# Summing the carry matrices' addends on VectorE, and making the second memory layer's operand earlier

## The chip, the cores and the metric

The kernel runs on one core of one Trainium2 chip. The core has a matrix engine (TensorE; PE in the profile, with its weight loads as PEld), a vector engine (VectorE, DVE), an activation engine (ScalarE, ACT), a general engine (GpSimd, POOL) and SyncE (SP), whose queue issues most transfers. Each engine works through its own instructions in order and waits for the others by semaphores. The metric is the device time of one execution, in microseconds; lower is better.

## The reference

One inference step of a two-layer streaming encoder. Layer 0 mixes tokens by an S5 state-space block, layer 1 by retention; each layer then attends to a memory and ends in a convolutional feed-forward block. Everything is float32. 512 prompt tokens and 32 sample tokens of width 1024 go through it. The change lies in two pieces:

```python
def s5_mixer(h, st_re, st_im, chunk, ...):
    a_bar, b_bar, c = s5_discretise(...)          # complex, 64 groups x 64 states
    ...
    # per group: x_t = a_bar * x_(t-1) + b_bar u_t ;  y_t = Re(c x_t) + d u_t
    g = jax.nn.gelu(y)
    out = g * jax.nn.sigmoid(g @ w_glu + b_glu)

def memory_kv(mem, g_mem, w_kv):                  # for each of the two layers
    m = rms_norm(mem, g_mem) @ w_kv               # mem: 256 tokens x 1024
    k, v = jnp.split(m, 2, axis=-1)
```

The memory keys and values of both layers depend on the memory tokens alone, and not on the encoder's progress.

## The kernel before, in words

The first stage (`phase1`) computes the S5 block and, between its parts, the memory keys and values of both layers. The stages after it (GLU, attention, feed-forward, retention, attention, feed-forward, final norm) aren't touched.

**S5.** The tokens are grouped by eight. Within eight tokens the recurrence is a matrix M per group; across them a carried state S is scanned. The 64 groups are handled in eight blocks of eight. For a block `e`, `powers` (letter V, line 813) makes operands on VectorE (lines 827 and 828) and GpSimd (829), `matrices` (M, 832) transposes them on TensorE (841), copies them by ScalarE (842), and builds M: Fg (853), copied into M by eight transfers (856). `states` (S, 858) multiplies the inputs on TensorE (867) and rotates the result on VectorE (882 to 886) and GpSimd. `scan` (Z, 892) runs the recurrence (900) and forms S (902 to 910); ScalarE copies its last columns out (912, 913). `carry` (C, 915) makes, for each half of a block, two products of 128x512 on VectorE, `y` (926) and `yt` (928): the two addends of the matrix by which the carried state is multiplied. `outputs` (O, 932) accumulates three products for each group on TensorE: M by the inputs (940), and S by `y` and by `yt` (942). ScalarE applies the activation (943), TensorE transposes (951), ScalarE copies the result into `g32` (953, 954).

**Memory keys and values.** `kv_units` (441) is a generator of 32 units, 16 for each layer: eight of keys (`keys`, 530) and eight of values (`values`, 553). Ahead of a layer's first unit stands `operand` (481): it loads the memory tokens in four transfers (450), and ScalarE scales them by the layer's gain. Layer 0's products are float32 (497, 528). Layer 1's operands are split into two parts that TensorE multiplies three times (240 to 242); its operand therefore takes eight ScalarE instructions (491) and eight VectorE instructions (492). Each unit loads a weight tile of 512 KB (520, or 226 with a rest that GpSimd's queue adds, 235).

**The order.** `fill(us)` draws units from the generator until their costs (3.5 us for each, 0 for an operand) have used up a credit. A prologue and then, for each block, a list written out by hand call the steps and fills in turn:

```python
PROLOGUE = (("V", 0), ("P", 0), ("M", 0), ("V", 1), ("S", 0), ("C", 0), ("Z", 0), ("M", 1), ("V", 2), ("F", 6))
ORDER = (("S", 1), ("C", 1), ("V", 3), ("Z", 1), ("O", 0), ("F", 4), ("M", 2), ("F", 5))
```

The number in ORDER is added to the block's. This gives priorities; a scheduler then fixes each engine's order ahead of the run, by its own estimate of times, and takes an instruction of lower priority first where the higher one isn't ready in that estimate. Most temporary tiles (the memory operands, `yt`, the products of V, S and Z, `g32`) come from one pool of 28 buffers of 560 columns (`slot`, 191). `y` comes from another of eight (`xl`, 807).

Of the kernel before, what the change touches and what calls it, by code (L numbers as in the profile page):

```python
# [13 lines left out]
OP = mybir.AluOpType  # L14
# [3 lines left out]
P = 128  # L18
# [7 lines left out]
NM = 256  # L26
# [146 lines left out]
class Kernel:  # L173
# [267 lines left out]
    def kv_units(self):  # L441

        nc, io = self.nc, self.io
        raw, first, ahead = [], [], []

        def load(ahead=lambda: None):
            raw.clear()
            for n in range(4):
                m = self.slot(512)
                nc.sync.dma_start(out=m, in_=io["memT"][n // 2][:, (n % 2) * 512:(n % 2 + 1) * 512])  # L450
                raw.append(m)
                if n == 1:
                    ahead()

        sq = []

        def squares():
            for k in range(4):
                t = self.slot(512)
                nc.scalar.activation(out=t, in_=raw[k], func=AF.Square)  # L460
                sq.append(t)
            for t, o in ((sq[0], sq[1]), (sq[2], sq[3]), (sq[0], sq[2]), (sq[0][:, :NM], sq[0][:, NM:])):
                nc.gpsimd.tensor_tensor(out=t, in0=t, in1=o, op=OP.add)

        def rms():

            ps = self.bank()
            for b in range(2):
                nc.tensor.matmul(ps[:, NM + b:NM + b + 1], lhsT=sq[0][:, b * P:(b + 1) * P], rhs=self.ones[:, :1], start=True, stop=True)
            self.mc = self.sp.tile([P, 2], F32, tag="mc", name="mc")  # L470
            m, tmp = self.small(2, "mm"), self.small(2, "mt")
            nc.vector.tensor_scalar(out=m, in0=ps[:, NM:NM + 2], scalar1=1.0 / D, scalar2=EPS, op0=OP.mult, op1=OP.add)
            self.rsqrt_of(m, self.mc, tmp)
            self.mps = ps

        def row():
            self.along_row(self.mps, self.mc, [(0, P), (1, P)])
            self.mr = self.sp.tile([P, NM], F32, tag="mr", name="mr")
            nc.scalar.copy(self.mr, self.mps[:, :NM])

        def operand(l):

            load(lambda: ahead.append(weights(0, io["w_k"][0, 0])) if l == 0 else None)
            self.mem = []
            for k in range(KT):
                src = raw[k // 2][:, (k % 2) * NM:(k % 2 + 1) * NM]
                g = self.gains[:, 32 + l * KT + k:33 + l * KT + k]
                if l in KV_SPLIT:
                    p = self.slot(2 * NM, dt=F32R)
                    m = p[:, :NM], p[:, NM:]  # L490
                    nc.scalar.activation(out=m[0], in_=src, func=AF.Copy, scale=g)
                    nc.vector.scalar_tensor_tensor(out=m[1], in0=src, scalar=g, in1=m[0].bitcast(F32), op0=OP.mult, op1=OP.subtract)
                else:
                    if k % 2 == 0:
                        t = self.slot(2 * NM)
                    m = t[:, (k % 2) * NM:(k % 2 + 1) * NM]
                    nc.scalar.activation(out=m, in_=src, func=AF.Copy, scale=g)
                self.mem.append(m)

        def staged():  # L500
            t = "acc" if self.n % 2 else "rr"
            return self.main.tile([P, T], F32, tag=t, bufs=1, name=self.name(t))

        def source(l, i):
            return io["w_k"][l, i] if i < KT else io["w_v"][l, (i - KT) // 4, (i - KT) % 4]

        prep = {}

        def look(u):

            if KT * 2 <= u + 1 < KT * 4:
                self.weights_close(prep[u + 1])
            if KT * 2 <= u + 2 < KT * 4:
                prep[u + 2] = self.weights_open(source(1, u + 2 - 2 * KT))

        def weights(l, src, u=None):
            if l in KV_SPLIT:
                return prep.pop(u)[:2]
            w = self.main.tile([P, 1024], F32, tag="wr", bufs=3, name=self.name("wr"))
            nc.sync.dma_start(out=w, in_=src)  # L520
            return w

        def product(l, out, a, ca, b, cb, k):

            if l in KV_SPLIT:
                self.mm3(out, [x[:, ca] for x in a], [x[:, cb] for x in b], k == 0, k == KT - 1)
            else:
                nc.tensor.matmul(out, lhsT=a[:, ca], rhs=b[:, cb], start=k == 0, stop=k == KT - 1)  # L528

        def keys(l, m):  # L530
            look(16 * l + m)
            w = ahead.pop() if ahead else weights(l, io["w_k"][l, m], 16 * l + m)
            ps = self.bank()
            for k in range(KT):
                product(l, ps[:, :NM], w, slice(k * P, (k + 1) * P), self.mem[k], slice(0, NM), k)
            first.append((l, m, ps))
            if l == 0 and m == 0:
                squares()
            if l == 0 and m == KV_RMS:
                rms()  # L540
            if l == 0 and m == KV_ROW:
                row()
            if l or m >= KV_ROW:
                for a in first:
                    keys_out(*a)
                first.clear()

        def keys_out(l, m, ps):
            o = staged()[:, :NM]
            nc.vector.tensor_tensor(out=o, in0=ps[:, :NM], in1=self.mr, op=OP.mult)  # L550
            nc.sync.dma_start(out=io["kT"][l, m // 4, :, (m % 4) * NM:(m % 4 + 1) * NM], in_=o)

        def values(l, n, c, ps):
            if c == 0:
                ps.extend([self.bank(), self.bank()])
            look(16 * l + 8 + 4 * n + c)
            w = weights(l, io["w_v"][l, n, c], 16 * l + 8 + 4 * n + c)
            for k2 in range(2):
                k = 2 * c + k2
                for b in range(2):  # L560
                    product(l, ps[b], self.mem[k], slice(b * P, (b + 1) * P), w, slice(k2 * 512, (k2 + 1) * 512), k)
            if c == 3:
                for b in range(2):
                    o = staged()[:, :512]
                    nc.scalar.activation(out=o, in_=ps[b], func=AF.Copy, scale=self.mc[:, b:b + 1])
                    nc.sync.dma_start(out=io["v"][l, b, :, n * 512:(n + 1) * 512], in_=o)

        for l in range(2):
            yield 0, lambda l=l: operand(l)
            for m in range(KT):  # L570
                yield KV_US, lambda l=l, m=m: keys(l, m)
            for n in range(2):
                ps = []
                for c in range(4):
                    yield KV_US, lambda l=l, n=n, c=c, ps=ps: values(l, n, c, ps)


    def cmul(self, eng, o, a, b, t, eng2=None):
# [10 lines left out]
    def phase1(self, sp):  # L589
        nc, io = self.nc, self.io  # L590
        V, A, PL = nc.vector, nc.scalar, nc.gpsimd
# [323 lines left out]
        def carry(e):  # L915

            d = E[e]
            g0 = 8 * e
            ca = load("ca", [P, 2, 8, C], io["ca"][e].rearrange("p (r n c) -> p r n c", r=2, n=8), 2)
            d["Y"] = []  # L920
            for hh in range(2):
                y, yt = xl(512), self.slot(512)
                y4, yt4 = (a.rearrange("p (g l c) -> p g l c", g=4, l=L) for a in (y, yt))
                shy = [P, 4, L, C]
                gg = slice(g0 + 4 * hh, g0 + 4 * hh + 4)
                V.tensor_tensor(out=y4, in0=ca[:, 0, 4 * hh:4 * hh + 4].unsqueeze(2).to_broadcast(shy),
                                in1=art[:, gg].unsqueeze(3).to_broadcast(shy), op=OP.mult)
                V.tensor_tensor(out=yt4, in0=ca[:, 1, 4 * hh:4 * hh + 4].unsqueeze(2).to_broadcast(shy),
                                in1=ait[:, gg].unsqueeze(3).to_broadcast(shy), op=OP.mult)
                d["Y"].append((y, yt))  # L930

        def outputs(e):
            d = E[e]
# [2 lines left out]
            for hh in range(2):  # L936
                py = self.bank()
                for i in range(4):
                    o, g = py[:69, i * P:(i + 1) * P], 4 * hh + i
                    nc.tensor.matmul(o, lhsT=u[:, g, 1:70], rhs=M[:, :, g], start=True, stop=False)  # L940
                    for n, y in enumerate(Y[hh]):
                        nc.tensor.matmul(o, lhsT=S[:, g, 0:69], rhs=y[:, i * P:(i + 1) * P], start=False, stop=n == 1)  # L942
                A.activation(out=yg[:, :, 64 * hh:64 * hh + 64].rearrange("p l (g c) -> p g l c", g=4),
                             in_=py[:69].rearrange("p (g l c) -> p g l c", g=4, l=8), func=AF.Gelu_apprx_tanh)
            g32 = self.slot()
# [469 lines left out]
```

## Time and profile before

| | us |
|---|---|
| median of three runs (1886.03 to 1888.63) | 1886.94 |
| the profiled execution | 1885.01 |
| its span in the trace | 1883.0 |
| TensorE busy in the span | 1823.7 |
| VectorE busy | 1055.0 |
| ScalarE busy | 629.0 |
| GpSimd busy | 342.3 |

The span runs from the first to the last instruction of the trace. Busy time is the time in which an engine had at least one instruction in work. In the timelines a row gives start and length in microseconds, the engine, the line of the kernel, the operation, the tile written and the tiles read, the shapes and how many instructions are merged into the row; square brackets at the end hold the idle time of the engine just ahead and what ended it. A row on TensorE counts passes: one float32 product is two.

### The profile page before, as it was taken

The page shows a single profiled execution, that of the slowest core. Times are in us where ns is not written, and L with a number is a line of the kernel's source. Part 1 is how long each engine was busy: PE and PEld are TensorE (multiplying, and loading weights), DVE is VectorE, ACT ScalarE, POOL GpSimd, SP SyncE. Part 2 cuts the span into 40 slices and gives each one's busy share as a digit, 9 for nine tenths or more (in the row PEclk, how much of TensorE's full clock was granted, in tenths as well). Part 3 has the DMA queues.
Part 4 walks back from the last instruction along what each step waited for, and adds up shares of the span by engine and source line. Part 5 has one row for each costly group of instructions (what it writes and reads, how often), then busy time and mean ns, then how long its engine had stood idle before and what let it go on. Part 6 is the DMA issues. An engine that isn't in the chain of part 4 may idle for free.

```text
span 1883.0 us, 33026 instructions
## 1 busy us (share of the span) xinstructions
PE 1823.7 (97%) x13943; PEld 1737.9 (92%) x13943; DVE 1055.0 (56%) x1779; ACT 629.0 (33%) x933; POOL 342.3 (18%) x416
## 2 busy tenths in 40 slices
PE   8778999999999999999999999999999999999998
PEld 7468799999999999999899899998899999999997
DVE  8887766545535535555555645556554554453553
ACT  3234454433323323333123222223443332232333
POOL 4645410021202202220000100100101121120221
PEclk9979999999999999999999999999999999999999
DMA  6637753122222222222222122222311222222221
GB/s 235 194 99 181 175 175 107 68 98 79 90 90 85 83 91 90 81 92 85 82 85 96 68 91 73 91 79 89 125 68 61 86 90 83 86 85 96 90 72 68
DMA packets 68276, 186.43 MB, mean 99 GB/s; under 512 B 9184, under 2 KB 18784, under 8 KB 68128
## 3 DMA queue, kind: packets, MB, share of 16 engines
q1 hardware_dynamic: 65536, 175.79, 28.1%
q0 software_dynamic: 2304, 8.39, 2.5%
q8 instruction: 109, 1.79, 0.4%
q14 instruction: 39, 0.32, 0.1%
q10 hardware_dynamic: 288, 0.15, 0.0%
HBM read 171.16 MB, written 10.77 MB: 97 GB/s over the span
## 4 chain that ended last, share of the span: by engine, by line
PE 88%; DVE 5%; DMA 2%; ACT 2%; issue 1%; POOL 1%; SPq 1%; DVEq 0%; ACTq 0%; POOLq 0%
PE ps L249 75%; PE ps L240 2%; PE ps L241 2%; PE ps L242 2%; PE bank L942 1%; PE bank L528 1%; DMA wr<-in_w_v 1%; DMA r<-in_memT 1%; PE ps L1339 1%; DVE wl L209 1%; PE bank L940 1%; POOL u L819 1%; PE ps L1328 0%; DMA wr<-in_w_k 0%; PE bank L742 0%
## 5 line engine op out<-in xcount | busy, mean ns | idle before, releaser
L249 PE MATMUL ps<-xh,wh 128*128 128x272 f32 x2432 | 505.7, 289 | 5.4 <-DVE x L372 3.5
L249 PE MATMUL ps<-xh,wl 128*128 128x272 f32 x2432 | 504.1, 289 | 0.0
L249 PE MATMUL ps<-xl,wh 128*128 128x272 f32 x2432 | 502.8, 288 | 0.0
L208 ACT CAST wh<-wr 128x1024 fp32r<-128x1024 f32 (+1 forms) x240 | 248.1, 1038 | 757.3 <-PE ps L249 639.7
L249 PE MATMUL ps<-r,wh 128*128 128x272 f32 x2688 | 447.8, 288 | 3.0 <-ACT r L954 1.6
L249 PEld LDWEIGHTS ps<-xh,wh 128*128 128x128 f32 x2432 | 382.4, 189 | 11.1 <-ACT r L314 3.7
L249 PEld LDWEIGHTS ps<-r,wh 128*128 128x128 f32 x2688 | 379.2, 188 | 6.4 <-ACT r L208 3.0
L249 PEld LDWEIGHTS ps<-xh,wl 128*128 128x128 f32 x2432 | 381.6, 189 | 2.3 <-issue 2.3
L249 PEld LDWEIGHTS ps<-xl,wh 128*128 128x128 f32 x2432 | 382.3, 188 | 0.3
L209 DVE TENSOR_TENSOR wl<-wr,wh 128x1024 fp32r<-128x1024 f32 (+1 forms) x240 | 296.2, 1237 | 93.2 <-ACT wh L208 85.2
L249 PE MATMUL ps<-r,wl 128*128 128x272 f32 x1344 | 277.7, 288 | 0.0
L249 PEld LDWEIGHTS ps<-r,wl 128*128 128x128 f32 x1344 | 210.6, 188 | 0.0
L372 DVE TENSOR_TENSOR x<-ps,x 128x544 f32<-128x544 f32 x96 | 69.3, 724 | 234.7 <-PE ps L249 234.5
L317 POOL TENSOR_TENSOR acc<-acc,r 128x544 f32<-128x544 f32 x36 | 59.2, 1645 | 455.1 <-ACT r L314 446.6
L1148 DVE TENSOR_TENSOR r<-ps,rr 128x544 f32<-128x544 f32 x44 | 31.9, 724 | 95.5 <-PE ps L249 95.5
L1138 DVE TENSOR_TENSOR r<-ps,rr 128x272 f32<-128x272 f32 x44 | 19.4, 442 | 116.9 <-PE ps L249 116.9
L1141 POOL COPY nco<-r 128x2 f32<-128x2 f32 x44 | 13.0, 295 | 373.4 <-DVE r L1139 373.4
L208 ACT CAST r<-r 128x544 fp32r<-128x544 f32 x84 | 52.5, 650 | 65.5 <-POOL r L1149 25.9
L1149 POOL TENSOR_TENSOR r<-r,r 128x32 f32<-128x32 f32 x44 | 35.2, 800 | 206.1 <-ACT wh L208 190.9
L1199 POOL TENSOR_TENSOR r<-r,r 128x544 f32<-128x544 f32 x8 | 10.8, 1356 | 339.4 <-ACT wh L208 325.5
L1146 DVE SCALAR_TENSOR_TENSOR r<-r,conv,r 128x546 f32<-128x546 f32 x88 | 69.1, 786 | 3.5 <-ACT r L1144 1.9
L209 DVE TENSOR_TENSOR r<-r,r 128x544 fp32r<-128x544 f32 x84 | 59.3, 729 | 12.4 <-ACT r L208 12.3
(348 smaller groups left out, 2127.1 us busy)
## 6 DMA issues: line engine op xcount, KB each, us to landing
wr<-in_w_r SPq DMA_DIRECT2D x48, 512.0 KB, 3.2
wr<-in_w_a SPq DMA_DIRECT2D x44, 512.0 KB, 3.2
wr<-in_w_g SPq DMA_DIRECT2D x44, 512.0 KB, 3.2
wr<-in_w_d SPq DMA_DIRECT2D x32, 448.0 KB, 3.3
wr<-in_w_k SPq DMA_DIRECT2D x16, 512.0 KB, 4.4
wr<-in_w_v SPq DMA_DIRECT2D x16, 512.0 KB, 3.7
wr<-in_w_q SPq DMA_DIRECT2D x16, 512.0 KB, 3.7
wr<-in_w_o SPq DMA_DIRECT2D x16, 512.0 KB, 3.3
```

The costliest lines, as they stand in the source:

```text
L208: self.nc.scalar.copy(hi, src)
L209: (self.nc.gpsimd if pool else self.nc.vector).tensor_tensor(out=lo, in0=src, in1=hi.bitcast(F32), op=OP.subtract)
L240: mm(out, lhsT=a[0], rhs=b[0], start=start, stop=False)
L241: mm(out, lhsT=a[0], rhs=b[1], start=False, stop=False)
L242: mm(out, lhsT=a[1], rhs=b[0], start=False, stop=stop)
L249: mm(ps[:, h, :TH], lhsT=ws[wi], rhs=x[xi][:, h * TH:(h + 1) * TH], start=start and n == 0, stop=stop and n == 2)
L317: add.tensor_tensor(out=self.acc, in0=self.acc, in1=sq, op=OP.add)
L372: self.nc.vector.tensor_tensor(out=self.halves(x), in0=src, in1=self.halves(x), op=OP.add)
L1138: V.tensor_tensor(out=ext[:, 2:2 + TH], in0=pa[:, 0, :TH], in1=r[:, :TH], op=OP.mult)
L1146: V.scalar_tensor_tensor(out=cv, in0=ext[:, t:t + W], scalar=cw[:, t, f:f + 1], in1=cv, op0=OP.mult, op1=OP.add)
L1148: V.tensor_tensor(out=self.halves(gr), in0=pg[:, :, :TH], in1=self.halves(r), op=OP.mult)
L1149: PL.tensor_tensor(out=gr[:, TP:], in0=gr[:, TP:], in1=cv[:, TP + 2:W], op=OP.mult)
```

## The change

Two edits. First, `carry` adds `yt` to `y` on VectorE (in place of the pair that was kept in line 930; the addition is called line 930 in the prediction, by the numbers of before), and `outputs` multiplies S by the sum alone: two products for each group instead of three. Second, `operand(1)` is drawn from the generator behind the first of layer 0's last four units (the thirteenth unit) instead of behind the sixteenth; so that both operands can exist at once, they are kept in a list by layer. By the credits it is now drawn in the fill that ends the prologue, where it was drawn in the last fill of block 0. The units themselves and their fills are the same.

```diff
-        raw, first, ahead = [], [], []
+        raw, first, ahead, mems = [], [], [], []
...
         def operand(l):
 
             load(lambda: ahead.append(weights(0, io["w_k"][0, 0])) if l == 0 else None)
-            self.mem = []
+            mems.append([])
...
-                self.mem.append(m)
+                mems[l].append(m)
...
+        yield 0, lambda: operand(0)
         for l in range(2):
-            yield 0, lambda l=l: operand(l)
             for m in range(KT):
                 yield KV_US, lambda l=l, m=m: keys(l, m)
             for n in range(2):
                 ps = []
                 for c in range(4):
                     yield KV_US, lambda l=l, n=n, c=c, ps=ps: values(l, n, c, ps)
+                    if l == 0 and n == 1 and c == 0:
+                        yield 0, lambda: operand(1)
...
-                d["Y"].append((y, yt))
+                V.tensor_tensor(out=y, in0=y, in1=yt, op=OP.add)
+                d["Y"].append(y)
...
                     nc.tensor.matmul(o, lhsT=u[:, g, 1:70], rhs=M[:, :, g], start=True, stop=False)
-                    for n, y in enumerate(Y[hh]):
-                        nc.tensor.matmul(o, lhsT=S[:, g, 0:69], rhs=y[:, i * P:(i + 1) * P], start=False, stop=n == 1)
+                    nc.tensor.matmul(o, lhsT=S[:, g, 0:69], rhs=Y[hh][:, i * P:(i + 1) * P], start=False, stop=True)
```

`keys` and `values` read `mems[l][k]` where they read `self.mem[k]`.

More of the change, by code (lines that the diff above doesn't have):

```diff
@@ L534, in keys @@
             for k in range(KT):
-                product(l, ps[:, :NM], w, slice(k * P, (k + 1) * P), self.mem[k], slice(0, NM), k)
+                product(l, ps[:, :NM], w, slice(k * P, (k + 1) * P), mems[l][k], slice(0, NM), k)
             first.append((l, m, ps))
@@ L560, in values @@
                 for b in range(2):
-                    product(l, ps[b], self.mem[k], slice(b * P, (b + 1) * P), w, slice(k2 * 512, (k2 + 1) * 512), k)
+                    product(l, ps[b], mems[l][k], slice(b * P, (b + 1) * P), w, slice(k2 * 512, (k2 + 1) * 512), k)
             if c == 3:
```

## The prediction

> **What bounds the kernel now.** I read the page first, for how full TensorE is over the whole span.
>
> ```profile
> span 1883.0 us, 33026 instructions
> PE 1823.7 (97%) x13943; PEld 1737.9 (92%) x13943; DVE 1055.0 (56%) x1779; ACT 629.0 (33%) x933; POOL 342.3 (18%) x416
> ```
>
> 97% is an average. Both edits lie in the first stage (S5 and memory projections), so I next read the windows view, cut where that stage ends and where VectorE starts the state products of a new block of eight groups (line 882). Columns: window, length, busy time of PE, PEld, DVE, ACT and POOL, granted clock, DMA share, GB/s.
>
> ```profile
> 87.00:113.00 26.00, 9.83 (x81) 8.55 (x81) 25.25 (x34) 6.25 (x16) 17.02 (x19) 0.70 0.60 152
> 113.00:122.40 9.40, 6.17 (x41) 5.05 (x41) 2.10 (x6) 2.48 (x7) 0.40 (x1) 0.50 0.33 89
> 122.40:144.50 22.10, 21.42 (x195) 19.87 (x196) 18.57 (x30) 11.41 (x20) 10.86 (x12) 0.90 0.43 107
> 144.50:164.20 19.70, 15.26 (x169) 14.12 (x167) 15.76 (x24) 7.77 (x16) 10.60 (x13) 1.00 0.75 192
> 164.20:184.10 19.90, 19.22 (x179) 17.60 (x175) 16.77 (x25) 9.03 (x18) 11.60 (x13) 0.91 0.66 156
> 184.10:203.50 19.40, 17.16 (x153) 14.56 (x151) 15.54 (x21) 8.44 (x17) 11.70 (x13) 1.00 0.77 188
> 203.50:219.65 16.15, 15.54 (x140) 13.05 (x136) 11.05 (x16) 9.08 (x18) 6.90 (x9) 1.00 0.71 179
> 219.65:240.60 20.95, 17.93 (x151) 16.32 (x149) 13.44 (x20) 10.06 (x23) 5.64 (x7) 1.00 0.70 193
> 240.60:1883.00 1642.40, 1624.76 (x12485) 1575.73 (x12485) 863.53 (x1405) 537.61 (x762) 219.62 (x276) 1.00 0.26 87
> ```
>
> From 240.60 on PE is 99% busy and the change touches nothing there: I count that part unchanged. Before it the bound alternates. From 87 to 113 VectorE is 97% busy and PE 38%. From 113 to 122.4 nobody is busy: a stall. Then come blocks where PE is full (122.4 to 144.5, 164.2 to 184.1) and blocks where it is not (77% and 88%) while VectorE, with 15 to 17 us of work in 20, forms a ring: line 882, the block's VectorE work up to line 909, ScalarE's copies, PE's state products (867), line 882 again.
>
> The stall I followed through the timelines of SyncE's queue, ScalarE, PE and VectorE (start, length, engine, line).
>
> ```profile
> 74.95 6.34 SPq L856 DMA_DIRECT2D M<-Fg  x8
> ...
> 104.62 0.95 SPq L450 DMA_DIRECT2D r<-in_memT  x2
> 111.80 6.21 SPq L856 DMA_DIRECT2D M<-Fg  x8
> 118.10 1.01 SPq L450 DMA_DIRECT2D r<-in_memT  x2
> ```
> ```profile
> 112.61 0.20 ACT L912 COPY stout<-r 128x8 f32<-128x8 f32 x1 [8.55 <-DVE r L909]
> ...
> 112.82 1.71 ACT L491 ACTIVATE r<-r,gains 128x256 fp32r<-128x256 f32 x4
> 121.45 1.71 ACT L491 ACTIVATE r<-r,gains 128x256 fp32r<-128x256 f32 x4 [6.92 <-DMA r<-in_memT]
> ```
> ```profile
> 113.38 0.58 PE L240 MATMUL bank<-r,wh 128*128 128x256 f32 x1 [9.99 <-ACT r L491]
> 113.89 1.90 PE L867 MATMUL bank<-u,xl 128*64 128x70 f32 x26
> ```
> ```profile
> 87.05 1.38 DVE L900 TENSOR_TENSOR_SCAN r<-d,r 128x280 f32<-128x280 f32 x2 [4.66 <-POOL r L888]
> ...
> 111.69 0.89 DVE L909 TENSOR_TENSOR r<-r 64x280 f32<-64x280 f32 x2
> 113.36 1.69 DVE L492 SCALAR_TENSOR_TENSOR r<-r,gains,r 128x256 fp32r<-128x256 f32 x4 [0.79 <-ACT r L491]
> 121.99 0.48 DVE L492 SCALAR_TENSOR_TENSOR r<-r,gains,r 128x256 fp32r<-128x256 f32 x1 [6.94 <-ACT r L491]
> 122.39 0.44 DVE L882 TENSOR_TENSOR r<-bank,ph 128x280 f32<-128x280 f32 x1
> ...
> 123.11 1.27 DVE L492 SCALAR_TENSOR_TENSOR r<-r,gains,r 128x256 fp32r<-128x256 f32 x3
> ```
>
> In these rows the second half of the memory tokens is issued at 118.10, behind eight copies of Fg into M that hold the queue for 6.21 us; ScalarE's second four scalings wait for it, VectorE's fifth split waits for those, and the S5 work of line 882 stands behind that split on VectorE, though PE ran the state products that it reads from 113.89.
>
> **The change part by part.** *The operand of layer 1.* Everything between VectorE's line 909, which ends at 111.69 + 0.89 = 112.58, and line 882 at 122.39 is this operand: 9.8 us, plus 1.27 us of splits behind it, 11.1 us. It is 0.79 + 6.94 = 7.7 us of waiting and 1.69 + 0.48 + 1.27 = 3.4 us of work. The change emits it at the fill that ends the prologue, ahead of block 1's state products. What moves is four loads (0.95 + 1.01 us of SyncE's queue), eight scalings on ScalarE (3.4 us) and eight splits on VectorE (3.4 us), with twelve of the 28 shared buffers. The loads pass the third set of Fg copies (111.80) and, depending on the scheduler, those at 74.95 too; behind them on SyncE come weights, ca and cbd, later by up to 2 us, which a 9.99 us idle PE covers. The waiting goes in either case. The work is free only if the splits fall into VectorE's 4.66 us wait ahead of the scan at 87.05; if they come after it they sit in the stretch that is 97% busy. The nearest row is the load that stands behind eight Fg copies, and copies stand at 74.95 as well, until 81.29. So I take the work as merely moved. Term A: **-7.7 us**, with bounds of -11.1 (hidden) and 0 (the loads are late again).
>
> *The addition.* It is sixteen instructions of 128x512 from SBUF to SBUF on VectorE, two for each block. No such addition stands in the trace; the nearest rows are the products of the same shape.
>
> ```profile
> L928 DVE TENSOR_TENSOR r<-ca,ait 128x512 f32<-128x512 f32 x16 | 22.3, 1431 | 0.0
> L829 POOL TENSOR_TENSOR r<-r,r 128x512 f32<-128x512 f32 x12 | 18.8, 1569 | 9.7 <-DVE r L828 9.7
> ```
> ```profile
> 127.39 0.68 DVE L827 TENSOR_TENSOR r<-Pr,bbr 128x512 f32<-128x512 f32 x1
> 128.00 0.68 DVE L828 TENSOR_TENSOR r<-PIn,bbi 128x512 f32<-128x512 f32 x1
> ```
>
> One product follows another after 0.61 us where GpSimd does not read beside it, and takes 1.43 us on average (line 928) where it does. The addition comes right behind 928 and ahead of 827, and GpSimd is mostly waiting there for VectorE (9.7 us of waits before line 829). I take 0.6. Block 0's pair has the 4.66 us wait as cover, and costs 1.2 us if the splits use that up. The other fourteen lie on the ring: 14 x 0.6 = 8.4 us. Behind each pair wait lines 827 and 900, and through them GpSimd's sums and the next state products. Term B: **+8.4 us**, with bounds of 0 (all in waits) and 14 x 1.43 = +20.0.
>
> Here the Trainium skill has a rule that speaks against the change: "SBUF — State Buffer", section "Who interferes with whom", says that a VectorE instruction with two SBUF inputs and a GpSimd instruction that reads SBUF exclude each other, the later one waiting to the other's end. By it every addition that meets a GpSimd operation costs what line 928 does, and the term would be near its upper bound.
>
> *The matmuls.* 64 products go (8 blocks x 8 groups), each two passes on PE, 128 records:
>
> ```profile
> L942 PE MATMUL bank<-r,r 128*69 128x128 f32 x128 | 25.4, 282 | 0.0
> ```
> ```profile
> 130.12 0.38 PE L942 MATMUL bank<-r,r 128*69 128x128 f32 x2
> 130.34 0.38 PE L940 MATMUL bank<-M,u 128*69 128x128 f32 x2
> ...
> 232.46 0.38 PE L942 MATMUL bank<-xl,r 128*69 128x128 f32 x2
> ```
> ```profile
> 139.56 1.06 ACT L842 COPY xl<-bank 128x512 f32<-128x512 f32 x2
> 179.95 1.06 ACT L842 COPY xl<-bank 128x512 f32<-128x512 f32 x2
> ```
> ```profile
> 143.71 1.20 PE L867 MATMUL bank<-u,xl 128*64 128x70 f32 x32
> 183.32 1.19 PE L867 MATMUL bank<-u,xl 128*64 128x70 f32 x32
> ```
> ```profile
> 230.16 0.92 DVE L909 TENSOR_TENSOR r<-r 64x280 f32<-64x280 f32 x2
> ```
>
> One takes 130.34 - 130.12 = 0.22 us of PE, eight in a block 1.74, all 64 14.0. That shortens the time only where PE is what is late. In the block to 144.5 the copies are done at 140.62 and PE starts 867 at 143.71: late by 3.1. In the block to 184.1: 181.01 against 183.32, late by 2.3. With 1.2 us more on VectorE and 1.74 less on PE these blocks change by the later of the two, max(1.2 - 3.1, -1.74) = -1.7 and max(1.2 - 2.3, -1.74) = -1.1, where term B has +1.2 for each: relief of 2.9 and 2.3. At the end, the last block's outputs start at 232.24 (232.46 less one product) though line 909 is done at 231.08: PE was late by about 1.2, which swallows that block's additions, and its eight removed products shorten the tail by 1.74: 2.9. Term C: **-8.1 us**, with bounds of 0 and -14.0.
>
> The sum is -7.7 + 8.4 - 8.1 = -7.4. The profiled execution took 1885.01 us (span 1883.0 and 2.0 around it), so 1877.6. It lay 1.9 below the median of the three runs shown, 1886.94; on that median I expect **1879.5 us**.
>
> **The rivals.** *Both edits pay in full* (1867.7): the splits hide in the 4.66 us wait (A -11.1), and with buffers freed at once the additions slide into VectorE's waits (B 0); C stays -8.1; together -19.2. For it: VectorE has 3 to 5 us without work in each block from 144.5 on. Against it: those waits are short and follow line 909, while 928 has stood behind 882 and 885 in each block so far, so that the additions would too.
>
> *The operand is still late* (1887.2): the change does not do what it says. The twelve buffers aren't free, or the scheduler leaves loads behind Fg copies, as now. A is 0, and B + C = +0.3. For it: two loads of one operand were issued 13.5 us apart. Against it: line 930 gives its second buffer back at once, where it was held until the outputs.
>
> *VectorE becomes the bound* (1890.9, slower): GpSimd's reads stand in the way of the additions, each costs the 1.43 us of line 928, 2.86 for each pair. B is +20.0; C is -8.3, because PE is then never late (3.1 + 2.3, and 1.2 + 1.74 at the end); A -7.7; together +4.0. The point at which it decides is an addition of 0.6 + 7.4 / 14 = 1.13 us on the path. For it: 928's mean. Against it: GpSimd's idle time before 829. That is the rule of the skill quoted above.
>
> **How the numbers follow.** Chances: forecast 0.53, both in full 0.22, operand late 0.15, VectorE bound 0.10. The range 1867 to 1889 takes in the forecast, the first two rivals and the lower side of the third. 0.2%, what a measurement of this kernel can tell, is 3.8 us, so faster means below 1883.2: 0.48 from the forecast's case and 0.22 from the first rival, 0.70; the same takes 0.05 of the forecast's case and 0.13 of the late operand's, 0.18; slower 0.12. The forecast's own case reaches from 1874 to 1885.
>
> **What would show it.** In the changed profile the loads of in_memT should all be issued before about 95 us, no wait for line 491 should stand on PE or VectorE near 113, line 930 should show sixteen instructions of about 0.7 us, line 942 no records of the second addend (128 now), and the first matmul of line 249 should come near 233 instead of 240.6, with the rest still 1642 us long. I am wrong if 930's mean is over 1.1 us, if a wait for in_memT remains, if the stage from 240.6 on changes its length by several us, or if blocks grow by more than 1.2 us with ScalarE or SyncE named as what they wait for.

## The result and the profile after

| | before | after |
|---|---|---|
| median, us | 1886.94 (5 runs) | 1877.61 (5 runs) |
| profiled execution, us | 1885.01 | 1877.61 |
| span, us | 1883.0 | 1875.8 |

The ratio is 0.9945, with a 95% interval of 0.9933 to 0.9958. At 1887 us that is 10.4 us less (7.9 to 12.6), and the medians differ by 9.3. The forecast was 1879.5, 7.4 less.

From line 576 on, the changed kernel's line numbers are two higher (three between the edit of `carry` and that of `outputs`): the sum is line 932, the product by S is 944, the state products are 869, the products for `y` and `yt` 928 and 930. First the windows view of the changed kernel, cut at the end of the first stage (window, length, busy time of PE, PEld, VectorE, ScalarE, GpSimd, granted clock, DMA share, GB/s):

```profile
0.00:233.61 233.61, 189.81 (x1330) 152.79 (x1331) 199.67 (x391) 91.32 (x172) 123.26 (x140) 0.91 0.66 183
233.61:1875.80 1642.19, 1624.17 (x12485) 1575.14 (x12485) 863.26 (x1405) 537.61 (x762) 219.44 (x276) 1.00 0.26 87
```

The first stage ends at 233.61 instead of 240.60, and the rest takes 1642.19 us as against 1642.40. In these two executions nearly all of the gain is in the first stage.

The loads of the second layer's operand, from the timelines of SyncE's queue, PE and VectorE after the change:

```profile
76.25 6.04 SPq L858 DMA_DIRECT2D M<-Fg  x8
...
84.39 2.77 SPq L450 DMA_DIRECT2D r<-in_memT  x4
```
```profile
110.88 0.58 PE L241 MATMUL bank<-r,wh 128*128 128x256 f32 x1 [5.25 <-DVE r L492]
...
119.94 0.69 PE L944 MATMUL bank<-xl,r 128*69 128x128 f32 x2 [6.35 <-DVE r L912]
```
```profile
83.60 2.94 DVE L932 TENSOR_TENSOR xl<-xl,r 128x512 f32<-128x512 f32 x2
88.35 1.37 DVE L902 TENSOR_TENSOR_SCAN r<-d,r 128x280 f32<-128x280 f32 x2 [1.80 <-POOL r L890]
...
98.21 1.37 DVE L492 SCALAR_TENSOR_TENSOR r<-r,gains,r 128x256 fp32r<-128x256 f32 x2 [0.52 <-ACT r L491]
100.27 0.48 DVE L492 SCALAR_TENSOR_TENSOR r<-r,gains,r 128x256 fp32r<-128x256 f32 x1 [0.69 <-ACT r L491]
...
110.35 1.66 DVE L492 SCALAR_TENSOR_TENSOR r<-r,gains,r 128x256 fp32r<-128x256 f32 x4
```

And PE's second wait for the operand before the change, which the prediction did not show:

```profile
122.01 0.58 PE L240 MATMUL bank<-r,wh 128*128 128x256 f32 x1 [2.85 <-ACT r L491]
```

All four loads are now issued together, behind the copies of Fg at 76.25 but ahead of the next ones. VectorE's waits for line 491 shrank from 0.79 + 6.94 to 0.52 + 0.69 us. The splits did not find the wait ahead of the first scan. They stand at 98 to 112, where VectorE is full, and PE still waits 5.25 us for the last of them. VectorE's wait ahead of the first scan fell from 4.66 to 1.80, because block 0's additions (2.94 us) stand in it. PE also has a new wait, of 6.35 us for line 912. Together with the 5.25 that is 11.6 us, where it waited 9.99 and 2.85 us for the operand before: what became shorter here is VectorE's chain rather than PE's idle time.

The additions, in the groups view of the changed kernel between 70 and 240.6 us (busy us, mean ns), and one block of them in VectorE's and GpSimd's rows:

```profile
L831 POOL TENSOR_TENSOR r<-r,r 128x512 f32<-128x512 f32 x12 | 19.5, 1625 | 8.0 <-DVE r L830 7.9
L932 DVE TENSOR_TENSOR xl<-xl,r 128x512 f32<-128x512 f32 x16 | 16.4, 1058 | 0.0
```
```profile
145.65 1.78 DVE L830 TENSOR_TENSOR r<-PIn,bbr 128x512 f32<-128x512 f32 x1
147.35 2.37 DVE L932 TENSOR_TENSOR xl<-xl,r 128x512 f32<-128x512 f32 x2
147.51 1.66 POOL L831 TENSOR_TENSOR r<-r,r 128x512 f32<-128x512 f32 x1 [0.63 <-DVE r L830]
149.64 1.36 DVE L902 TENSOR_TENSOR_SCAN r<-d,r 128x280 f32<-128x280 f32 x2
```

In three of the eight blocks, of which the rows show one, the additions do not stand right behind `yt` as I had assumed, but behind the products of the `powers` step, and GpSimd's sum (831) starts beside the first of them. A pair takes 2.4 us there instead of the 1.2 that I had put down. In the last two blocks, where VectorE has no such products, a pair stands right behind `yt` and takes 1.28 us. Over all sixteen the mean is 1.06 us, close to the 1.13 at which I had said that the gain would be gone. The gain was not gone, which is what the experiments had to explain.

VectorE's timeline after the change also has a wait for a staging buffer's transfer, which I had not counted on:

```profile
160.57 0.42 DVE L550 TENSOR_TENSOR acc<-bank,mr 128x256 f32<-128x256 f32 x1 [3.04 <-DMA out_kT<-acc]
```

### The profile page after: what moved, and what is told of

The parts are those of the page before. It is cut to its first block, busy times and chain, and to the rows that moved or that the text cites. A ratio compares the mean times of both kernels' runs of the same rounds, so it can differ in the third digit from the quotient of the medians.

```text
span 1875.8 us, 32777 instructions
## 1 busy us (share of the span) xinstructions
PE 1814.0 (97%) x13815; PEld 1727.9 (92%) x13815; DVE 1062.9 (57%) x1795; ACT 628.9 (34%) x933; POOL 342.7 (18%) x416
## 4 chain that ended last, share of the span: by engine, by line
PE 85%; DVE 8%; DMA 2%; issue 2%; ACT 2%; POOL 1%; SPq 0%; DVEq 0%; ACTq 0%; POOLq 0%
PE ps L249 75%; PE ps L240 2%; PE ps L241 2%; PE ps L242 2%; DMA M<-Fg 1%; DMA wr<-in_w_v 1%; PE ps L1341 1%; DVE r L902 1%; POOL u L821 1%; DVE r L830 1%; DVE wl L209 0%; PE ps L1330 0%; DVE r L930 0%; ACT wh L208 0%; PE ps L1303 0%
## 5 line engine op out<-in xcount | busy, mean ns | idle before, releaser
L209 DVE TENSOR_TENSOR r<-r,r 128x544 fp32r<-128x544 f32 x84 | 59.3, 728 | 10.6 <-ACT r L208 10.4
```

Of the source, the lines that this page charges most:

```text
L209: (self.nc.gpsimd if pool else self.nc.vector).tensor_tensor(out=lo, in0=src, in1=hi.bitcast(F32), op=OP.subtract)
```

## The experiments

My theory was the sum of three terms: the operand -7.7, the additions +8.4, the matmuls -8.1. The rivals were that TensorE is the bound throughout (additions free, matmuls worth 14), and that VectorE is (matmuls free, additions 8 to 20). Each run was timed against the kernel before on the same chip. The fourth column is the ratio's distance from 1, times 1887 us, with its interval. The last two are of the one profiled execution of each kernel: where its first stage ends (the first matmul of line 249), and how long the rest takes. They show where a difference lies, but each is a single execution; that of the doubled additions was the fastest of its kernel, 1882.44 us.

| kernel | median, us | ratio | against before, us | first stage ends, us | rest, us |
|---|---|---|---|---|---|
| before | 1886.94 | 1 | | 240.60 | 1642.4 |
| the change | 1877.61 | 0.9945 | -10.4 (-12.6 to -7.9) | 233.61 | 1642.2 |
| addition alone | 1884.75 | 0.9983 | -3.2 (-4.9 to -1.5) | 239.74 | 1642.1 |
| operand alone | 1880.81 | 0.9967 | -6.2 (-8.7 to -4.0) | 235.54 | 1642.7 |
| every addition twice | 1885.83 | 0.9990 | -1.9 (-3.6 to -0.2) | 237.59 | 1643.0 |
| 64 products more | 1886.03 | 0.9991 | -1.7 (-3.4 to 0.0) | 240.45 | 1644.3 |
| a second, tiny addition | 1877.61 | 0.9938 | -11.7 (-14.0 to -9.2) | 232.40 | 1644.5 |
| additions on GpSimd | 1884.49 | 0.9976 | -4.5 (-6.6 to -2.6) | 239.40 | 1642.1 |
| operand five units earlier | 1880.80 | 0.9953 | -8.9 (-11.3 to -6.6) | 234.20 | 1645.3 |
| operand two units earlier | 1879.18 | 0.9948 | -9.8 (-12.3 to -7.5) | 235.20 | 1643.9 |
| no additions | 1876.06 | 0.9941 | -11.1 (-13.4 to -8.9) | 230.96 | 1643.0 |
| staging buffers in turn | 1875.91 | 0.9938 | -11.7 (-14.3 to -9.2) | 228.19 | 1645.9 |
| carry first | 1872.16 | 0.9914 | -16.2 (-18.5 to -14.0) | 225.52 | 1642.4 |
| carry first, buffers in turn | 1869.42 | 0.9900 | -18.9 (-21.3 to -16.4) | 225.97 | 1642.3 |

### Each half of the change alone

The addition alone is the kernel before with these lines:

```diff
-                d["Y"].append((y, yt))
+                V.tensor_tensor(out=y, in0=y, in1=yt, op=OP.add)
+                d["Y"].append(y)
...
-                    for n, y in enumerate(Y[hh]):
-                        nc.tensor.matmul(o, lhsT=S[:, g, 0:69], rhs=y[:, i * P:(i + 1) * P], start=False, stop=n == 1)
+                    nc.tensor.matmul(o, lhsT=S[:, g, 0:69], rhs=Y[hh][:, i * P:(i + 1) * P], start=False, stop=True)
```

> The addition alone: y and yt are summed on VectorE and TensorE gets one product, while the second layer's operand stays where it was before. Theory (three terms: operand -7.7, additions +8.4, matmuls -8.1): additions and matmuls cancel, so 1885 to 1889 us, ratio 0.999 to 1.001. Rival 1, TensorE is the bound and additions are free: 8 to 14 us faster than before, 1873 to 1879. Rival 2, VectorE is the bound and the matmuls were free: about 8 us slower, 1895; with each addition blocked by GpSimd 15 to 20 us slower.

The operand alone is the changed kernel with these lines put back as they were.

> The operand alone: the second layer's operand is drawn behind the thirteenth unit, and TensorE still gets both addends. Theory: only the wait goes, 1886.9 - 7.7 = 1879.2, between 1876 (its work hidden too) and 1881. Rival 1 (TensorE the bound): the 12.8 us that TensorE waited go, less what it waits elsewhere, 1874 to 1877. Rival 2 (the operand gains little by itself, because the sixteen buffers held by yt keep the loads late): 1885 to 1888.

Measured: -3.2 and -6.2 us. They add up to -9.4, and both together gave -10.4: intervals of some 2 us to either side show nothing between the halves. The operand's term is close to what was forecast, and the rival that it gains little by itself is out. The addition's half was to be zero and is not. Its interval excludes zero, but it also excludes the 8 to 14 us of a TensorE bound throughout. In the profile of the addition alone the operand's two halves come together and late, and PE has one wait of 18.09 us where it had 9.99 and a second, shorter one of 2.85:

```profile
120.79 0.58 PE L240 MATMUL bank<-r,wh 128*128 128x256 f32 x1 [18.09 <-ACT r L491]
```

### The additions twice, and a tiny one

```diff
                 V.tensor_tensor(out=y, in0=y, in1=yt, op=OP.add)
+                V.tensor_tensor(out=yt, in0=y, in1=yt, op=OP.add)
                 d["Y"].append(y)
```

> The changed kernel with every addition made twice (the second sum goes into yt, which nothing reads): sixteen more instructions of 128x512 on VectorE. Theory: 14 x 0.6 = +8.4 us over the changed kernel, 1886. If GpSimd blocks each of them, +14 to +20, 1892 to 1898. If the additions lie in VectorE's waits or TensorE is the bound, +0 to 2, 1878 to 1880.

The control has the same line with `[:, :8]` on all three operands.

> The changed kernel with a second addition of only 8 columns behind each (into yt, which nothing reads): the same number of instructions and dependences as with every addition made twice, hardly any of their length. If the price of the additions is their length on VectorE, +0 to 2 us over the changed kernel, 1878 to 1880. If what the doubled additions cost came from the other order that the scheduler made of one more instruction, as much as there, +8, 1886.

Measured: sixteen more additions cost 8.5 us over the change (-1.9 against -10.4), sixteen more tiny ones nothing (-11.7). So the price comes with the length on VectorE, and not with the number of instructions. That the longer additions cost in part through another order isn't excluded, since the scheduler goes by estimated times. By the medians a second addition costs 0.53 us, near the 0.6 that I had put down for the first. In the profiled execution the doubling moved the end of the first stage by 4.0 us only.

### No additions at all

```diff
-                V.tensor_tensor(out=y, in0=y, in1=yt, op=OP.add)
                 d["Y"].append(y)
```

> The changed kernel without the additions: yt is still made, TensorE multiplies S by y alone, and so this kernel leaves the second addend out of its result. Its time shows the two terms by themselves. Theory: 8.4 us faster than the changed kernel, 1869, and 8 us faster than the kernel with the operand alone. Since the addition alone was 3 us faster than before, and not equal, a term is too large: if the additions cost less, 1871 to 1874, with the matmuls worth 8; if the matmuls are worth more, 1869 and 11.

Measured: -11.1, as against -10.4 with the additions. By these figures the first sixteen cost 0.7 us, with some 3 us to either side, and the second sixteen 8.5. The ends of the first stage show it less unequal, 2.7 and 4.0 us. Neither number that I expected came (1869, or 1871 to 1874). The windows view shows a part of the reason. It is cut from the first block's scan to the last block's scan; the fifth entry, without the counts, is VectorE's busy time. In this order: no additions, the change, and every addition twice.

```profile
88.29:217.42 129.13, 103.50 (x884) 89.94 (x885) 107.97 (x159) 56.87 (x109) 74.39 (x82) 0.87 0.68 167
```
```profile
88.35:221.70 133.35, 102.98 (x889) 90.43 (x889) 115.64 (x172) 57.79 (x110) 73.27 (x82) 0.86 0.69 168
```
```profile
88.12:224.43 136.31, 102.27 (x885) 90.25 (x886) 126.05 (x186) 56.60 (x108) 77.21 (x82) 0.87 0.67 162
```

The additions of the change put 7.7 us of work on VectorE (107.97 to 115.64), but its idle time falls from 21.2 to 17.7, and the stretch grows by 4.2 in these single executions. Doubling them puts on 10.4 more, idle time falls to 10.3, and the stretch grows by 3.0. VectorE does not set the pace alone in any of the three: it waits 8 to 16% of the time, and work that is added to it goes into those waits in part.

Two more things stand in the timelines. Here are VectorE's rows without the additions, then one row of the change.

```profile
101.91 0.88 DVE L492 SCALAR_TENSOR_TENSOR r<-r,gains,r 128x256 fp32r<-128x256 f32 x2 [3.30 <-ACT r L491]
...
119.96 0.45 DVE L884 TENSOR_TENSOR r<-bank,ph 128x280 f32<-128x280 f32 x1
...
147.14 2.40 DVE L902 TENSOR_TENSOR_SCAN r<-d,r 128x280 f32<-128x280 f32 x2
```
```profile
117.89 0.45 DVE L884 TENSOR_TENSOR r<-bank,ph 128x280 f32<-128x280 f32 x1
```

First, where no addition stands beside GpSimd's sum, the scan (902) does, and takes 2.40 us; behind the additions it took 1.36. So the additions' own rows in this stretch, 13.5 us (16.4 less block 0's 2.94), put only 7.7 on VectorE. Second, without the additions the operand's scalings and splits come in another order, and the third block's state products (884) start 2.1 us later. From there to the last block's scan this kernel needs 6.4 us less than the change, of which the three blocks in the middle, from one start of line 884 to the next, give 0.5, 0.9 and 0.5 us where I had put 1.2 for each; behind that scan it needs 1.6 us more. The small difference at the end is a balance of these, and not the price of the additions by itself. What the runs bear out is that they cost between nothing and 4 us beside the shorter work of TensorE, not 8.4.

### The matmuls put back

```diff
+                    nc.tensor.matmul(o, lhsT=u[:, g, 1:70], rhs=M[:, :, g], start=True, stop=True)
                     nc.tensor.matmul(o, lhsT=u[:, g, 1:70], rhs=M[:, :, g], start=True, stop=False)
```

> The changed kernel with the product of M by the inputs made twice for each group (the second starts the sum anew, so the result is the same): TensorE gets as many passes as before the change, with nothing else changed. Theory: +8.1 us over the changed kernel, 1885.7. If TensorE is never late, 0, 1877.6. If TensorE is the bound throughout, +14.0, 1891.6.

Measured: 8.7 us over the change, with the additions in place. From the operand alone to the kernel without additions the same 64 products go while there are no additions: 4.9 us (-6.2 to -11.1). Together the four kernels form a square (the products put back are by M, those taken out by S; they have the same size). Products are worth 8.7 us where VectorE also adds and 4.9 where it doesn't; additions cost 4.5 us where PE has all its products (-6.2 to -1.7) and 0.7 where it hasn't. The ends of the first stage give the same pattern, less marked: 6.8 and 4.6 for the products, 4.9 and 2.7 for the additions. The intervals of the differences are some 3 us to either side, so that this pattern is likely and not settled. It fits two engines that take turns in being late: either alone has slack, both together have not. 14.0, TensorE bound throughout, is out.

### GpSimd for the additions

The edit puts `PL.` for `V.` in the addition.

> The changed kernel with the additions on GpSimd instead of VectorE. Theory (VectorE's ring is what the additions lengthen): VectorE gets its 8 us back, but GpSimd takes about 1.57 us for each (line 829 of the kernel before), 3.1 a block, and holds off VectorE's products meanwhile: 1872 to 1878. Rival (VectorE is not the bound): no gain, or slower by GpSimd's time, 1880 to 1895.

Measured: -4.5, so 5.9 us slower than on VectorE. The gain that theory gave did not come. Here is the groups view of that kernel:

```profile
L932 POOL TENSOR_TENSOR xl<-xl,r 128x512 f32<-128x512 f32 x16 | 25.0, 1644 | 1.3 <-DVE r L930 1.3
...
L829 DVE TENSOR_TENSOR r<-Pr,bbr 128x512 f32<-128x512 f32 x6 | 10.4, 1732 | 0.0
L830 DVE TENSOR_TENSOR r<-PIn,bbi 128x512 f32<-128x512 f32 x6 | 10.3, 1714 | 0.0
```

VectorE's products beside it take 1.73 and 1.71 us; in the profile before the change their rows showed 0.68. VectorE is relieved of 16.4 us of additions, and yet it is busy for 207.67 us in the first stage, 8.0 more than in the change: beside GpSimd its other work takes that much longer. This is the rule of the Trainium skill that the prediction weighed ("SBUF — State Buffer", section "Who interferes with whom": with two SBUF inputs on VectorE and reads on GpSimd, the later one waits). The trace agrees: 1.7 us beside GpSimd, 0.7 away from it.

### The operand earlier still

The edits move the drawing of `operand(1)` behind the eighth unit, and behind the eleventh.

> The changed kernel with the second layer's operand drawn behind the eighth unit (the last of the first layer's keys), five units earlier. Theory: its 3.4 us of splits leave the stretch in which VectorE is full, if they find VectorE idle earlier: 3.4 us faster than the changed kernel, 1874. If its twelve buffers are missed by the S5 steps before, or the splits only push other work of VectorE, 1877 to 1882.

> The changed kernel with the second layer's operand drawn behind the eleventh unit, two units earlier. Theory as for the eighth unit: up to 3.4 us faster than the changed kernel, 1874 to 1878; if the loads' place in SyncE's queue behind the copies of Fg decides, the loads come ahead of them and the wait of TensorE at 110.9 us goes.

Measured: -8.9 and -9.8; no gain, and perhaps a loss of 1 us. Here are the splits and the first block's scan of the first of these kernels, then the windows of the changed kernel at the time where the splits now stand.

```profile
L492 DVE SCALAR_TENSOR_TENSOR r<-r,gains,r x8: 468/475/482, 27.6 to 33.4; 128x256 fp32r<-128x256 f32 x8
```
```profile
92.41 1.36 DVE L902 TENSOR_TENSOR_SCAN r<-d,r 128x280 f32<-128x280 f32 x2
```
```profile
20.00:50.00 30.00, 28.10 (x114) 22.27 (x113) 29.62 (x95) 4.51 (x8) 11.07 (x14) 0.94 0.55 193
50.00:70.00 20.00, 20.00 (x75) 10.57 (x74) 19.86 (x36) 3.08 (x5) 11.45 (x8) 1.00 0.63 198
```

The splits did move, to 27.6 to 33.4 us, and PE's wait for line 492 is gone. But VectorE is 99% busy there as well (29.62 of 30 us, 19.86 of 20), and the first scan starts at 92.41 instead of 88.35. So the splits push other work of VectorE, which was the second of the two reasons that I had given for no gain. The 3.4 us are not to be had in this way.

### The staging buffers, and the carry step first

The prediction's first rival had the additions sliding into VectorE's waits. I tried to bring that about.

```diff
-            t = "acc" if self.n % 2 else "rr"
+            turns[0] += 1
+            t = "acc" if turns[0] % 2 else "rr"
```

> The changed kernel with the two staging buffers of the memory outputs taken in turn, where a count of names now picks them and often takes the same one twice. In the changed profile VectorE waits 0.7 and 3.0 us (line 550) for such a buffer's transfer. Theory (VectorE's ring is the bound, so a wait on it counts): 2 to 4 us faster than the changed kernel, 1874 to 1876. Rival (the wait only fills a gap in which VectorE has to wait for TensorE anyway): 1877 to 1878.

```diff
-ORDER = (("S", 1), ("C", 1), ("V", 3), ("Z", 1), ("O", 0), ("F", 4), ("M", 2), ("F", 5))
+ORDER = (("C", 1), ("S", 1), ("V", 3), ("Z", 1), ("O", 0), ("F", 4), ("M", 2), ("F", 5))
```

> The changed kernel with the carry step ahead of the state products in the order by hand, so that its four products and two additions have the right of way into VectorE's wait ahead of line 882. Theory: they fill the 3 us of wait of each block from the third on, 5 to 15 us faster than the changed kernel, 1863 to 1873. Rival (they push the ring's own start back by their 5 us instead): slower, 1880 to 1890.

> The changed kernel with both the buffers in turn and the carry step first. If the two act on different waits, the sum of their effects; if they fill the same wait of VectorE, the larger of the two alone.

Measured: -11.7, -16.2 and -18.9. By their times the buffers alone are not told apart from the change (1.3 us, within the interval). In the profiled execution VectorE's wait of 3.04 us is gone and the first stage ends 5.4 us earlier, but the rest takes 3.7 us longer than in the change, which the last section comes back to. The carry step first is told apart: its interval (-18.5 to -14.0) lies below that of the change. Here is VectorE's timeline of that kernel over one wait:

```profile
169.42 0.90 DVE L911 TENSOR_TENSOR r<-r 64x280 f32<-64x280 f32 x2
170.35 0.42 DVE L550 TENSOR_TENSOR rr<-bank,mr 128x256 f32<-128x256 f32 x1
170.69 1.28 DVE L930 TENSOR_TENSOR r<-ca,ait 128x512 f32<-128x512 f32 x2
171.89 1.28 DVE L928 TENSOR_TENSOR xl<-ca,Pr 128x512 f32<-128x512 f32 x2
173.10 1.28 DVE L932 TENSOR_TENSOR xl<-xl,r 128x512 f32<-128x512 f32 x2
174.30 0.41 DVE L550 TENSOR_TENSOR rr<-bank,mr 128x256 f32<-128x256 f32 x1
176.15 0.29 DVE L855 TENSOR_TENSOR Fg<-bank,Fg 128x128 f32<-128x128 f32 x1 [1.43 <-PE bank L851]
176.82 0.45 DVE L884 TENSOR_TENSOR r<-bank,ph 128x280 f32<-128x280 f32 x1 [0.39 <-PE bank L869]
```

All six instructions of the carry step now stand in the wait between the end of a block (911) and the start of the next (884), the additions too, and with GpSimd out of the way a pair of any of them takes 1.28 us. In the changed kernel `yt` and the additions stood behind line 884, on the ring. What moved is the whole step, `yt` too, and not the additions alone. With the buffers in turn as well the median is the lowest of the study, 1869.42 us, 0.9900 of before (0.9887 to 0.9913), 8 us below the change. It is not told apart from the carry step first alone (2.7 us, some 3 to either side). The first stage ends at 225.97 with both and at 225.52 with the carry step alone, so that the buffers add nothing there: the two seem to fill the same waits of VectorE, as far as single executions tell.

## Why the prediction was right, and where it was not

**The sign and the sum** held: -7.4 forecast, -9.3 by the medians and -10.4 by the ratio, inside the range and below the bound for "faster". The stage view held too: line 249's first matmul, which I had put near 233, came at 233.61, and the rest stayed at 1642 us.

**Term A**, the operand, was put at -7.7 and measured alone -6.2 (-8.7 to -4.0). Its mechanism is in the rows: the loads are together, VectorE's waits of 7.7 us became 1.2, and the splits were merely moved into the full stretch, as I took it. The bound of -11.1 was not reached by drawing the operand still earlier. My note that no wait for line 491 would remain was too strong: VectorE keeps two short ones, and PE has one of 5.25 us for line 492. "Nobody is busy" from 113 to 122.4 was a misreading: in the row that I quoted PE is busy for 6.17 of 9.40 us, at half the clock.

**Terms B and C** are where the prediction failed, and they have to be read together. The prediction said "The other fourteen lie on the ring: 14 x 0.6 = 8.4 us", and then C gave back what PE's lateness swallows of them in two blocks and at the end. So by its own rule the additions cost 4 x 1.2 = 4.8 us while PE has all its products, and 5.5 us once they are gone (the sum of B and C, 0.3, plus the 3 x 1.74 that the products alone would give). The products are worth 3 x 1.74 = 5.2 us without additions, and 4.5 beside them. Measured, in the same order: 4.5, 0.7, 4.9 and 8.7 us. Where only additions come in, or only products go, the rule fits. With both, the result is better than the rule gives: B and C together were put at +0.3 and measured as -3.2 (the addition alone) and -4.2 (the change less the operand alone), 3.5 to 4.5 us too dear.

The step that failed is that four blocks of the ring pay 1.2 us each for their additions whatever PE does, with PE late only in two blocks and at the end. In the three middle blocks the additions made a block longer by 0.5 to 0.9 us, though a pair took 2.4 us there and not 1.2; one reason is in the rows, the scan that became shorter behind it. I had treated each block's VectorE work as a closed loop, though the windows that I quoted showed VectorE idle for 3 to 5 us in most blocks. How much of the missing price lies in those waits, and how much in the scheduler's other order, stays open.

So A was 1.5 us too generous, and B and C together were 3.5 to 4.5 too dear. These errors offset each other in part. That the sum came within 2 to 3 us of the measurement is partly luck, and no proof of its terms.

**The rivals.** That the operand is still late fell with the operand alone. That VectorE becomes the bound fell with the missing price of the additions; its point of decision, 1.13 us an addition, was a price on the path, and the profile's 1.06 us was only in part on the path. That both pay in full was nearest in its mechanism for the additions, and the order with the carry step first came closest to it. Its sum was not consistent: with B at 0, C's own rule gives 3 x 1.74 = 5.2 us and not 8.1.

## What to carry to other kernels

The price of work added to an engine is not its length times its count where two engines take turns at being late: read the engine's idle time stage by stage, and expect added work to cost less than its length as long as there are waits to take it. Here the medians say that the first sixteen additions were far cheaper than the next sixteen; the profiled executions say so less clearly. A control with the same instructions at a negligible size separates their length from their number cheaply. Taking work out, as in the kernel without additions, can also change the scheduler's order elsewhere, so look at the timeline before calling the difference a price. And where a step has a natural wait to stand in, its place in the order by hand can be worth more than added work costs: here the place of the whole carry step was worth 6 us, and the additions cost between nothing and 5.

## What the runs showed of the hardware

TensorE's granted clock at the start of the stage after the first differed between executions of these kernels for no reason that the profile shows. Here are windows of 9 us before the stage's end and 6 us after it, first for the changed kernel, then for the one with the operand five units earlier, and then, behind the end alone, for the one with the staging buffers in turn:

```profile
224.61:233.61 9.00, 5.18 (x49) 4.46 (x48) 5.34 (x9) 6.08 (x17) 0.00 (x0) 1.00 0.50 160
233.61:239.61 6.00, 6.00 (x48) 6.00 (x49) 4.68 (x8) 3.69 (x7) 0.00 (x0) 1.00 0.99 338
```
```profile
225.20:234.20 9.00, 5.07 (x50) 4.40 (x48) 5.35 (x9) 6.10 (x17) 0.00 (x0) 0.92 0.52 165
234.20:240.20 6.00, 6.00 (x29) 6.00 (x30) 4.67 (x8) 3.66 (x7) 0.00 (x0) 0.56 1.00 348
```
```profile
228.19:234.19 6.00, 6.00 (x27) 6.00 (x28) 4.68 (x8) 3.68 (x7) 0.00 (x0) 0.52 0.99 327
```

PE was busy for 5.2 and 5.1 of the last 9 us. Then the one kept the full clock and ran 48 matmuls in 6 us, and the other ran 29 at 0.56. The 19 that are missing are 19 x 0.125 = 2.4 us at the pace of the first, and the rest of that execution took 1645.3 us instead of 1642.2. With the buffers in turn 27 ran, and the rest took 1645.9: most of what that kernel had gained in its first stage was gone again. Of the fourteen profiled executions six had a lower clock in these 6 us, 0.52 to 0.72. Five of them took 1643.9 to 1645.9 us for the rest; the sixth, with the additions on GpSimd, took 1642.1, as the eight at full clock did (1642.1 to 1643.0). So a lower clock there often comes with a longer rest, but not always. How busy PE was just before doesn't sort them: with the additions doubled it was busy for 4.06 of the 9 us and kept the clock, and with 64 products more it was busy for 6.80, with no wait over 1.6 us, and did not. The Trainium skill's page "TensorE: Matmul & The Clock Gate", section "Part 1: The HAM clock gate", says that the clock follows activity in a window that runs freely, so that the same kernel can meet it differently from run to run. These rows agree with that, though they are of different kernels.
